# The gate of the first half step on VectorE, and one more chunk in the seven-product form

## The chip, the cores and the metric

One core of one Trainium2 chip. The metric is the device time of one execution in microseconds (us); lower is better. Engines: TensorE (PE, its weight loads PEld), VectorE (DVE), ScalarE (ACT), GpSimd (POOL), SyncE (SP), which issues most transfers.

## The reference

A two-layer backbone over 512 latent tokens and 256 context tokens of width 1024. Each layer is a half SwiGLU step, a token mixer (neighbourhood attention in the first layer, windowed attention in the second) and another half step. Every sub-layer is modulated by vectors made from a conditioning vector, and closed by a layer norm:

```
m_lat = split(silu(c) @ w_mod[i] + b_mod[i], 9)        # context tokens: the same with c_ctx
y = swiglu(h * (1 + scale) + shift, w_in, w_out)       # (silu(a) * v) @ w_out, width 2816
h = layer_norm(ALPHA * h + 0.5 * gate * y)
```

There are four half steps, called 0a, 0b, 1a and 1b. The shift, scale and gate of 0a are the first three of the nine modulation vectors of layer 0 (rows 0 to 7, 8 to 15 and 16 to 23 in blocks of 128 outputs).

## The kernel before

Activations are kept transposed: 8 tiles `z` of 128 features by 768 tokens (512 latent, 256 context). Products are made in three passes, with each operand split into a high and a low part (`mm3`, L152): high by high, low by high, high by low. A weight quarter of 128x512 is loaded raw (`raw_quarter`, L92; five raw buffers), copied to the high part by ScalarE and subtracted to the low part by GpSimd (`split_w`, L100). High and low parts live in a ring of eight quarters each, two units of four.

**A half step** (`ffn`, L457) has 11 chunks of two units of 128 inner features. A plain chunk makes, for each unit f and each group of tokens (512 and 256), `pa` and `pv` (`av`, L465), multiplies `silu(pa)` by `pv` on VectorE, splits the result, and multiplies by the third unit, `down` (L489): 8 output tiles `pd` per group, each added into `z` with the gate as a factor by VectorE (`accumulate`, L452). So the gate must be there before the first addition. The down products of chunk 0 rotate over three banks, two of tag s and the one of tag t.

A chunk in the **seven-product form** (`seven`, L590) makes `pa` and `pv` of both halves of the tokens from seven products instead of eight, as in Strassen's scheme in Winograd's variant. It needs sums of the activations, made once (`sums`, L528, and `fourth`, L549; on VectorE, GpSimd and ScalarE), and sums of the weight quarters for every unit (`quarters`, L566: four additions and seven splits, nearly all on GpSimd). Its down weights are split another way (`adding=True`): ScalarE writes the high part and the negated one, and a transfer on GpSimd's queue adds the weights to it. Before the sums overwrite them, halves of the activations are saved to memory (`save`, L522) and later restored.

`s0` (L638) is the first chunk in that form: 3 in 0a, where the first products were opened already while the inputs came in, and 2 in the others. Chunk `s0 - 1` holds the sums. Chunks 9 and 10 are plain again.

**The modulation vectors** come in two ways. Those of shift and scale of 0a, and its gate, are made on TensorE (`gemv`, L164): weights as the moving operand against a 32-column conditioning operand, evicted and transposed by eight small products with `sel`. For the gate `late_gate` (L1237), called at the start of `ffn` as `mid()`, does two of these with 8 transfers each (`gemv_bg`, L185). All others are **row products on VectorE** (`gemv_dve`, L195): a tile of 128 outputs by 512 inputs is loaded, multiplied by the conditioning row, which lies in a PSUM bank (o for the latent stream, t for the context stream; copied there with Silu by ScalarE, L225), and summed in the same instruction (L208). A block of 128 outputs takes two halves and two streams, four products. They are a background list `bg`; `tick()` (L237) advances it by `pace[0]` steps at fixed places in the chunks. `weight` (L639) says how much each chunk is to take; chunk s0 - 1 takes none. In 0a the list has blocks 24 to 71 of layer 0: 192 products. Outside phase T their rows use the six buffers t2, as the gate's pieces do; in phase T two buffers and `zspare`.

**Order.** The program text gives an order of priority; a planner then simulates the engines and writes each engine's queue, so that an instruction ready early is moved ahead of later ones. Engines take their queues strictly in order. `behind` (L322) adds an order without a wait. `bias_tables` (L822), called at the end of chunk 1 of 0a, builds the attention bias in memory with 8 + 16 transfers of small pieces on SP's queue.

Of the kernel before, what the change touches and what calls it, by code (L numbers as in the profile page):

```python
# [38 lines left out]
def hybrid_kernel(ctx: ExitStack, tc: tile.TileContext, h0, cc, crow, wmod, wmodt, bmod, lnp, wst,  # L39
                  rpbp, nmask, sinks, ropec, rmat, ident, wmask, out):  # L40
    nc = tc.nc
# [8 lines left out]
    def bank(tag, nm):  # L50
        return pp.tile([P, 512], F32, tag=tag, name=nm, bufs=banks[tag])

    def t2(nm, tag="t2"):
        return tp.tile([P, 512], F32, tag=tag, name=nm, bufs={"t2": 6, "ln": 2, "sl": 2}[tag])
# [109 lines left out]
    def gemv(layer, ch, pieces, tag):  # L164

        nm = f"{layer}_{ch}"
        ps = bank(tag, f"gm{nm}")
        kt = 0
        for t in pieces:
            for j in range(t.shape[1]):  # L170
                q = kt % 4
                nc.tensor.matmul(ps[32 * q:32 * q + 32, :], c_sb[:, kt, :], t[:, j, :], start=kt < 4, stop=kt >= 4,
                                 tile_position=(0, 32 * q))
                kt += 1
        ev = t2(f"gev{nm}")
        nc.scalar.copy(ev[:], ps[:])
        pt = bank(tag, f"gt{nm}")
        for j in range(4):
            nc.tensor.matmul(pt[:, 2 * j:2 * j + 2], ev[:, j * P:(j + 1) * P], sel[:], start=True, stop=True)
        for a in range(2):  # L180
            t = ch * 2 + 8 * a if ch < 4 else ch * 4 + 2 * a
            nc.vector.tensor_tensor(out=mod[layer][:, t:t + 2, :], in0=pt[:, 4 * a:4 * a + 4].rearrange("p (t s) -> p t s", s=2),
                                    in1=bmod_sb[:, layer, t:t + 2, None].broadcast_to([P, 2, 2]), op=ALU.add)

    def gemv_bg(layer, ch):  # L185
        pieces = []
        for q in range(8):
            t = t2(f"wm{layer}_{ch}_{q}").rearrange("p (a b) -> p a b", a=1)
            nc.sync.dma_start(t[:], wmod[ch, q // 4, :, q % 4:q % 4 + 1, :])
            pieces.append(t)  # L190
        gemv(layer, ch, pieces, "o")

    bg, last, last_exp, wtq = [], [None], [None], [0]

    def gemv_dve(layer, *ranges):  # L195


        def products(t, half, cb, out):
            wtq[0] += 1
            nm = f"wt{layer}_{t}_{half}"  # L200
            if phase_of[0] != "T":
                w = t2(nm)
            else:
                w = zspare if wtq[0] % 3 == 0 else ph["T"].tile([P, 512], F32, tag="wt", name=nm, bufs=2)
            nc.sync.dma_start(w[:], wmodt[layer, t, half])
            for st in sorted(out):
                junk = t2(f"jk{layer}_{t}_{half}_{st}", "ln")
                x = nc.vector.tensor_tensor_reduce(out=junk[:], in0=w[:], in1=cb[st], scale=1.0, scalar=0.0,  # L208
                                                   op0=ALU.mult, op1=ALU.add, accum_out=out[st])
                behind(x, last[0])  # L210
                yield

        def steps():
            cb, now = {}, None
            for i, (t0, t1, streams) in enumerate(ranges):
                acc = tp.tile([P, 48, 2, 2], F32, tag="gacc", name=f"ga{layer}_{t0}", bufs=1)[:, 0:t1 - t0]
                for half in ((0, 1), (1, 0))[i % 2]:
                    if half != now:
                        now, cb = half, {}
                        for st in streams:  # L220
                            nm = f"cb{layer}_{t0}_{half}_{st}"
                            t = t2(nm, "ln")
                            nc.sync.dma_start(t[:], crow[st, half:half + 1, :].broadcast_to([P, 512]))
                            cb[st] = bank("ot"[st], nm)[:]
                            behind(nc.scalar.activation(cb[st], t[:], AF.Silu), last_exp[0])  # L225
                    for t in range(t0, t1):
                        yield from products(t, half, cb, {st: acc[:, t - t0, half, st:st + 1] for st in streams})
                n = len(streams)
                nc.vector.tensor_tensor(out=acc[:, :, 0, 0:n], in0=acc[:, :, 0, 0:n], in1=acc[:, :, 1, 0:n], op=ALU.add)
                nc.vector.tensor_tensor(out=mod[layer][:, t0:t1, 0:n], in0=acc[:, :, 0, 0:n],  # L230
                                        in1=bmod_sb[:, layer, t0:t1, None].broadcast_to([P, t1 - t0, n]), op=ALU.add)

        bg.append((sum(2 * len(st) * (t1 - t0) for t0, t1, st in ranges), steps()))

    pace = [0.0, 0.0]

    def tick():  # L237

        pace[1] += pace[0]
        while bg and pace[1] >= 1:  # L240
            pace[1] -= 1
            if next(bg[0][1], "end") == "end":
                bg.pop(0)
# [25 lines left out]
    def gate(layer, m, w):  # L269
        gt = cp.tile([P, DT, 2], F32, name=f"gt{layer}_{m}")  # L270
        nc.vector.tensor_scalar(out=gt[:], in0=mvec(layer, m), scalar1=w, scalar2=None, op0=ALU.mult)
        return gt
# [49 lines left out]
    def behind(x, y):  # L322

        if y is not None and x.ins.engine == y.ins.engine:
            tc.add_manual_dep(x.ins, y.ins.name, mybir.DependencyInfo(
                mybir.DependencyClass.NoSync, mybir.DependencyReason.DATA), reason="order")
# [130 lines left out]
    def ffn(nm, groups, gt, mid, post, units=(), opened={}, head=None, apart=None):  # L457
# [177 lines left out]
            mid()  # L635
        gts.append(gt())
        late_downs, js = [], []
        s0 = 3 if opened else 2  # L638
        weight = [0] + [1.0] * (s0 - 2) + [0] + [1.0] * (NCH - 2 - s0) + [1.2] * (s0 - 1)  # L639
        each = sum(n + 1 for n, _ in bg) / (sum(weight) - 0.1)  # L640
        for ci in list(range(NCH)) + [("r", NCH - 2)]:
# [57 lines left out]
            a, b = groups  # L699
# [116 lines left out]
    def constants():  # L816
        for t, src in ((lnp_sb, lnp), (nmask_sb, nmask), (rm_sb, rmat)):
            behind(nc.sync.dma_start(t[:], src[:]), loaded[0])
        nc.sync.dma_start(nsink[:], sinks[:].broadcast_to([P, NH]))
        nc.vector.tensor_scalar(out=nsink[:], in0=nsink[:], scalar1=-1.0, scalar2=None, op0=ALU.mult)  # L820
# [318 lines left out]
    first, opened = [], []  # L1139
# [14 lines left out]
    with tc.tile_pool(name="pre", bufs=1) as fp:  # L1154
        open_av()
        for q in range(4):
            pieces = []
            for i in range(2):
                t = fp.tile([P, 4, 512], F32, tag="wm", name=f"wm0_{q}_{i}", bufs=7)
# [75 lines left out]
            write(norm)  # L1235

    def late_gate():  # L1237
        for ch in (4, 5):
            gemv_bg(0, ch)
        constants()  # L1240

    def whole(x, head):

        return lambda gi: [f() for f in (x[:5] if gi == 0 else head)]
# [4 lines left out]
    l3 = [ln("l3", i, g, 1, 0, 1, 3, "o", True) for i, g in enumerate(g2)]  # L1249
    l4 = [ln("l4", i, g, 1, 1, 1, 6, ("mm", "o")[i]) for i, g in enumerate(g1)]  # L1250

    gemv_dve(0, (24, 40, (0, 1)), (40, 72, (0, 1)))
    ffn("0a", g2, lambda: gate(0, 2, 0.5), late_gate, whole(l0[0], l0[1][:1]), first,
        {(f, g): ps for f in range(2) for g, ps in zip(g2, opened[f])})
    plan(pq0_0_0=l0[1][1:2], pk0_1_0=l0[1][2:3], vn0_1=l0[1][3:5] + l0[0][5:] + l0[1][5:])
# [3 lines left out]
    gemv_dve(1, (0, 24, (0, 1)))  # L1259
    plan(pv0b_0_0_0=l1[1][1:2], pv0b_0_1_0=l1[2][2:3], pd0b_0_0_4=l1[2][3:], pd0b_0_0_7=l1[1][2:3], pa0b_0_0_512=l1[1][3:])  # L1260
    ffn("0b", g2, lambda: gate(0, 8, 0.5), None, whole(l2[0], l2[1][:1]), head=[g3[0], g3[2], g3[1]], apart=True)
    gemv_dve(1, (24, 40, (0, 1)), (40, 72, (0,)))
    plan(pa1a_0_0_0=l2[0][5:], pa1a_0_1_0=l2[1][1:2], pd1a_0_0_1=l2[1][2:3], pd1a_0_0_4=l2[1][3:])
    ffn("1a", g2, lambda: gate(1, 2, 0.5), None, whole(l3[0], l3[1][:1]), apart=True)
    plan(vw_3=l3[1][1:2], wk1=l3[1][2:3], wq0_0=l3[1][3:5] + l3[0][5:] + l3[1][5:])
    plan(wo6_3=l4[0][:1], wo7_2=l4[0][1:2], pow3_1_256_2=l4[0][2:3], pow3_1_256_6=l4[0][3:5], pow3_1_256_7=l4[1][:1])
# [129 lines left out]
```

## Time and profile before

| what | value |
|---|---|
| time, three runs | 2860.63 us median (2854.68 to 2862.81) |
| profiled execution | 2868.23 us, span 2866.4 us |
| busy: PE, DVE, POOL, ACT | 95%, 63%, 58%, 42% |
| mean granted TensorE clock | 0.972 |
| bytes moved | 322.42 MB, mean 112 GB/s |

A row of the timeline gives start and length in us, engine, line, operation, output <- inputs, sizes, count, and in brackets how long the engine was idle before it and what ended that. A row of the windows gives a stretch of the span, its length, the busy time of PE, PEld, DVE, ACT and POOL (with counts), the granted clock, the share of the transfer engines, and GB/s.

### The profile page before, as it was taken

Reading aid. Unit: us, or ns where it says so; the run is one execution under the profiler, and the core shown is the slowest. Engines: PE = TensorE matmul, PEld = TensorE weight load, DVE = VectorE, ACT = ScalarE, POOL = GpSimd, SP = SyncE. Lnnn points to the kernel's source line nnn. Section 1 sums busy time; section 2 is a strip of 40 time slices with the busy share of each in tenths; the row PEclk is TensorE's granted clock in tenths of the full one; section 3 lists DMA queues with packets and bytes.
Section 4 is the critical chain, followed back from the end, with each engine's and each line's share of the span. In section 5 each row is a group of like instructions: output and inputs, shape, how many; then the busy total and the mean of one; then the engine's idle time right before and its main releaser. Section 6 shows DMA issues by size and latency. Waiting matters only on the chain.

```text
span 2866.4 us, 48106 instructions
## 1 busy us (share of the span) xinstructions
PE 2728.1 (95%) x17122; PEld 2447.8 (85%) x17122; DVE 1805.4 (63%) x4124; ACT 1213.4 (42%) x2497; POOL 1658.0 (58%) x1488
## 2 busy tenths in 40 slices
PE   8999999999999989999999999999998998899997
PEld 5789899888888878999998899998886776888997
DVE  3286777585545676766654776666566667687744
ACT  4223333256454444434333534343246555444443
POOL 4357575375434455876744677765466444577763
PEclk9999999999999989999999999999999999899998
DMA  8525557432212212345462326466522111235562
GB/s 300 141 87 158 133 144 208 134 103 82 60 49 62 58 56 86 97 121 140 119 167 83 96 83 166 134 183 180 174 81 62 31 31 45 59 89 129 123 181 65
DMA packets 286016, 322.42 MB, mean 112 GB/s; under 512 B 28497, under 2 KB 174033, under 8 KB 284753
## 3 DMA queue, kind: packets, MB, share of 16 engines
q1 hardware_dynamic: 269936, 290.89, 34.2%
q0 software_dynamic: 15552, 28.32, 5.9%
q8 instruction: 135, 2.21, 0.3%
q14 instruction: 105, 0.85, 0.1%
q10 hardware_dynamic: 288, 0.14, 0.0%
HBM read 311.41 MB, written 12.25 MB: 113 GB/s over the span
## 4 chain that ended last, share of the span: by engine, by line
PE 52%; DVE 6%; DMA 2%; issue 2%; ACT 1%; POOL 1%; SPq 0%; DVEq 0%; POOLq 0%; ACTq 0%
PE pd1a L153 2%; PE pd0b L153 2%; PE pd1a L154 2%; PE pd0b L154 2%; PE pd0b L155 2%; PE pd1a L155 2%; PE wo L800 1%; PE pd1b L153 1%; PE pd1b L154 1%; PE pd1b L155 1%; DMA wr<-in_wst_dram 1%; PE tpw L791 1%; PE pa1a L153 1%; PE pa1a L154 1%; PE pv1a L153 1%
## 5 line engine op out<-in xcount | busy, mean ns | idle before, releaser
L104 POOL TENSOR_TENSOR wl<-wr,wh 128x512 fp32r<-128x512 f32 x308 | 404.0, 1328 | 298.4 <-ACT wh L102 238.4
L104 POOL TENSOR_TENSOR wl_s<-S,wh_s 128x512 fp32r<-128x512 f32 x202 | 268.4, 1366 | 60.5 <-ACT wh_s L102 59.7
L102 ACT CAST wh<-wr 128x512 fp32r<-128x512 f32 x308 | 186.7, 619 | 215.1 <-DMA wr<-in_wst_dram 62.2
L102 ACT CAST wh_s<-S 128x512 fp32r<-128x512 f32 x216 | 130.9, 620 | 322.4 <-POOL S L574 84.1
L208 DVE CUSTOM_DVE_ANT_0 jk<-wt,cb 128x512 f32<-128x512 f32 x303 | 200.4, 680 | 61.4 <-DMA wt<-in_wmodt_dram 52.1
L574 POOL TENSOR_TENSOR S<-wr,wr 128x512 f32<-128x512 f32 x108 | 146.9, 1360 | 148.6 <-DMA wr<-in_wst_dram 130.1
L104 POOL TENSOR_TENSOR wl_a<-wr,wh_a 128x512 fp32r<-128x512 f32 x120 | 159.1, 1376 | 24.9 <-ACT wh_a L102 24.5
L102 ACT CAST wh_a<-wr 128x512 fp32r<-128x512 f32 x162 | 100.4, 621 | 125.9 <-PE pd1b L154 18.3
L453 DVE SCALAR_TENSOR_TENSOR z<-pd0b,gt,z 128x256 f32<-128x256 f32 (+1 forms) x176 | 103.4, 602 | 62.2 <-PE pd0b L155 62.0
L453 DVE SCALAR_TENSOR_TENSOR z<-pd1a,gt,z 128x512 f32<-128x512 f32 (+1 forms) x168 | 99.8, 619 | 44.5 <-PE pd1a L155 43.3
L807 POOL TENSOR_SCALAR p<-p,l 128x512 f32<-128x512 f32 x64 | 44.6, 698 | 128.9 <-DVE l L906 120.5
L453 DVE SCALAR_TENSOR_TENSOR z<-pd0a,gt,z 128x512 f32<-128x512 f32 (+1 forms) x168 | 98.7, 618 | 29.5 <-PE pd0a L155 28.9
L319 POOL TENSOR_SCALAR z<-z,ag_None,ab_None 128x256 f32<-128x256 f32 (+1 forms) x78 | 63.5, 819 | 53.4 <-DVE uh L305 42.8
L208 DVE CUSTOM_DVE_ANT_0 jk<-zspare,cb 128x512 f32<-128x512 f32 x113 | 75.8, 679 | 15.6 <-DMA zspare<-in_wmodt_dram 15.6
L807 POOL TENSOR_SCALAR pw<-pw,l 128x512 f32<-128x512 f32 (+1 forms) x64 | 41.2, 645 | 74.4 <-DVE l L1097 33.0
L574 POOL TENSOR_TENSOR S<-S,wr 128x512 f32<-128x512 f32 x54 | 77.1, 1427 | 3.2 <-DVE x1b L557 0.7
L574 POOL TENSOR_TENSOR S<-wr,S 128x512 f32<-128x512 f32 x54 | 76.8, 1422 | 2.9
L905 ACT ACTIVATE p<-s,m 128x512 f32<-128x512 f32 x64 | 44.0, 688 | 77.3 <-DVE m L903 72.3
L453 DVE SCALAR_TENSOR_TENSOR z<-pd1b,gt,z 128x512 f32<-128x512 f32 (+1 forms) x98 | 56.8, 609 | 14.8 <-PE pd1b L155 12.3
L306 DVE TENSOR_TENSOR ul<-ufl,uh 128x256 fp32r<-128x256 f32 (+1 forms) x88 | 63.0, 722 | 2.3 <-ACT ufl L301 1.7
L301 ACT ACTIVATE ufl<-z,bi_None,sc_None 128x256 f32<-128x256 f32 (+1 forms) x86 | 54.7, 654 | 22.2 <-DVE z L438 21.9
L153 PE MATMUL pd0a<-gh0a,wh 128*128 128x512 f32 (+1 forms) x144 | 50.6, 365 | 8.3 <-DVE z L453 8.3
(1463 smaller groups left out, 10687.0 us busy)
## 6 DMA issues: line engine op xcount, KB each, us to landing
wr<-in_wst_dram SPq DMA_DIRECT2D x524, 256.0 KB
wt<-in_wmodt_dram SPq DMA_DIRECT2D x175, 256.0 KB
zspare<-in_wmodt_dram SPq DMA_DIRECT2D x65, 256.0 KB
wr_0b<-in_wst_dram SPq DMA_DIRECT2D x42, 256.0 KB
wr_1b<-in_wst_dram SPq DMA_DIRECT2D x42, 256.0 KB
wr_2b<-in_wst_dram SPq DMA_DIRECT2D x42, 256.0 KB
wr_3b<-in_wst_dram SPq DMA_DIRECT2D x42, 256.0 KB
wm<-in_wmod_dram SPq DMA_DIRECT2D x8, 1024.0 KB
```

The source lines that it names most:

```text
L102: nc.scalar.copy(hi[:], src[:])
L104: eng.tensor_tensor(out=lo[:], in0=src[:], in1=hi[:].bitcast(F32), op=ALU.subtract)
L153: nc.tensor.matmul(ps, a[0], b[0], start=first, stop=False)
L154: nc.tensor.matmul(ps, a[0], b[1], start=False, stop=False)
L155: last_pe[0] = nc.tensor.matmul(ps, a[1], b[0], start=False, stop=last)
L208: x = nc.vector.tensor_tensor_reduce(out=junk[:], in0=w[:], in1=cb[st], scale=1.0, scalar=0.0, op0=ALU.mult, op1=ALU.add, accum_out=out[st])
L301: nc.scalar.activation(uf[:, :n], zs, AF.Identity, scale=s1, bias=s2)
L306: return hi, nc.vector.tensor_tensor(out=lo, in0=uv, in1=uo.bitcast(F32), op=ALU.subtract)
L319: nc.gpsimd.tensor_scalar(out=zs, in0=zs, scalar1=prm[2][:, d:d + 1], scalar2=prm[3][:, d:d + 1], op0=ALU.mult, op1=ALU.add)
L453: last[0] = nc.vector.scalar_tensor_tensor(out=zt(d, c0, c1), in0=pd, scalar=gt[:, d, st:st + 1], in1=zt(d, c0, c1), op0=ALU.mult, op1=ALU ...
L574: nc.gpsimd.tensor_tensor(out=t[:], in0=a[:], in1=b[:], op=o)
L807: nc.gpsimd.tensor_scalar(out=p, in0=p, scalar1=r, scalar2=0.0, op0=ALU.mult, op1=ALU.add)
```

## The change

Two things change. The gate of 0a is made by `gemv_dve` (blocks 16 to 23, both streams: 32 products), all of it stepped at once in `late_gate`, and `gemv_bg` goes; the background list for blocks 24 to 71 is set up after it, still ahead of chunk 0. And `s0` is 2 in 0a too: chunk 2 takes the seven-product form, chunk 1 holds the sums and takes no background steps, and only chunk 9 instead of 9 and 10 takes them at the end.

```
-    def gemv_bg(layer, ch):
-        pieces = []
-        for q in range(8):
-            t = t2(f"wm{layer}_{ch}_{q}").rearrange("p (a b) -> p a b", a=1)
-            nc.sync.dma_start(t[:], wmod[ch, q // 4, :, q % 4:q % 4 + 1, :])
-            pieces.append(t)
-        gemv(layer, ch, pieces, "o")
...
-        s0 = 3 if opened else 2
+        s0 = 2
...
     def late_gate():
-        for ch in (4, 5):
-            gemv_bg(0, ch)
+        gemv_dve(0, (16, 24, (0, 1)))
+        pace[0] = 1
+        while bg:
+            tick()
         constants()
+        gemv_dve(0, (24, 40, (0, 1)), (40, 72, (0, 1)))
...
-    gemv_dve(0, (24, 40, (0, 1)), (40, 72, (0, 1)))
     ffn("0a", g2, lambda: gate(0, 2, 0.5), late_gate, whole(l0[0], l0[1][:1]), first,
```

## Rows read from the trace of the kernel before

**Rows 1.** The page, busy time of each engine over the whole span.

```profile
PE 2728.1 (95%) x17122; PEld 2447.8 (85%) x17122; DVE 1805.4 (63%) x4124; ACT 1213.4 (42%) x2497; POOL 1658.0 (58%) x1488
```

**Rows 2.** Windows: chunk 2 of 0a, plain, and a seven-product chunk (period).

```profile
161.90:212.10 50.20, 50.20 (x291) 44.28 (x290) 39.55 (x64) 15.90 (x32) 29.64 (x24) 1.00 0.20 61
...
332.90:378.80 45.90, 45.90 (x266) 43.92 (x265) 32.99 (x81) 17.55 (x32) 30.71 (x26) 1.00 0.56 148
```

**Rows 3.** Windows (PE, PEld, clock, DMA) for lines L172 and L179 alone.

```profile
63.00:106.00 43.00, 12.36 (x32) 1.77 (x32) 1.00 0.37 105
...
63.00:106.00 43.00, 1.90 (x16) 2.02 (x16) 1.00 0.37 105
```

**Rows 4.** Timeline of TensorE, around a gate pair and at the first down product.

```profile
63.61 1.05 PE L172 MATMUL gm<-wm,c_sb 128*32 128x512 f32 x2
64.59 0.38 PE L154 MATMUL pa0a<-ul,wh 128*128 128x256 f32 x1
...
74.70 0.39 PE L153 MATMUL pd0a<-gh0a,wh 128*128 128x512 f32 x1
```

**Rows 5.** Timelines of VectorE and SP, and windows, around the wait in chunk 1.

```profile
140.13 0.69 DVE L208 CUSTOM_DVE_ANT_0 jk<-wt,cb 128x512 f32<-128x512 f32 x1 [9.65 <-DMA wt<-in_wmodt_dram]
...
116.46 12.21 SPq L826 DMA_DIRECT2D yd<-xd  x14
129.53 0.87 SPq L205 DMA_DIRECT2D wt<-in_wmodt_dram  x1
...
135.00:142.00 7.00, 0.17 (x2) 0.11 (x1) 1.70 (x5) 0.00 (x0) 0.00 (x0) 0.66 0.89 286
142.00:150.00 8.00, 7.50 (x17) 5.44 (x18) 6.44 (x18) 2.13 (x4) 3.77 (x3) 0.50 0.82 259
```

**Rows 6.** Timelines of VectorE and SP: products back to back, change of half.

```profile
126.58 0.68 DVE L208 CUSTOM_DVE_ANT_0 jk<-wt,cb 128x512 f32<-128x512 f32 x1
127.19 0.08 DVE L208 DVE_READ_ACCUMULATOR2_ANT ga<- 128x1 f32 x1
...
233.32 0.42 SPq L223 DMA_DIRECT2D cb<-in_crow_dram  x1
...
240.40 0.69 DVE L208 CUSTOM_DVE_ANT_0 jk<-wt,cb 128x512 f32<-128x512 f32 x1 [1.90 <-ACT cb L225]
```

**Rows 7.** Timeline of VectorE when the gate is there, and the window before.

```profile
105.61 0.24 DVE L271 TENSOR_SCALAR gt<-mod 128x16 f32<-128x16 f32 x1
...
78.84:105.70 26.86, 26.86 (x142) 18.77 (x141) 2.79 (x9) 5.58 (x11) 8.32 (x8) 1.00 0.31 93
```

**Rows 8.** GpSimd: the page's group of a split, and an accumulate transfer's issue.

```profile
L104 POOL TENSOR_TENSOR wl_s<-S,wh_s 128x512 fp32r<-128x512 f32 x202 | 268.4, 1366 | 60.5 <-ACT wh_s L102 59.7
...
305.19 0.87 POOL L107 DMA_DIRECT2D wl_3b<-in_wst_dram  x1
```

**Rows 9.** Timelines and windows: the waits in chunks 3 and 4.

```profile
259.82 0.69 DVE L208 CUSTOM_DVE_ANT_0 jk<-zspare,cb 128x512 f32<-128x512 f32 x1 [4.34 <-DMA zspare<-in_wmodt_dram]
...
318.82 0.79 PE L153 MATMUL pd0a<-gh0a,wh_2b 128*128 128x512 f32 x1 [6.89 <-DVE gl0a L603]
...
306.48 8.37 DVE L260 TENSOR_TENSOR bi_None<-sc_None,lnp_sb 128x16 f32<-128x16 f32 x1
...
306.20:312.00 5.80, 5.72 (x26) 4.38 (x24) 5.80 (x2) 1.67 (x3) 5.80 (x5) 1.00 0.45 94
...
226.70:332.90 106.20, 95.68 (x529) 89.51 (x529) 77.98 (x173) 36.49 (x68) 67.72 (x57) 0.95 0.51 142
```

**Rows 10.** Windows: the turn to the seven-product form in 0b.

```profile
1150.00:1170.00 20.00, 18.84 (x109) 16.16 (x108) 19.76 (x34) 5.99 (x14) 10.26 (x9) 1.00 0.00 1
```

**Rows 11.** Groups of VectorE between 162 and 212 us: two kinds of sums.

```profile
L518 DVE TENSOR_TENSOR x0a<-x0a,ul 128x384 f32<-128x384 f32 x12 | 6.7, 560 | 0.2
L559 DVE TENSOR_TENSOR ul<-x0a,uh 128x384 fp32r<-128x384 f32 x4 | 4.4, 1119 | 0.0
```

**Rows 12.** Timeline of TensorE: the longest wait of the second mixer.

```profile
2435.59 0.58 PE L153 MATMUL pow<-woh,wh 128*128 128x256 f32 x1 [8.44 <-ACT pw L1084]
```

## The prediction, made before the changed kernel was run

> **What bounds the kernel now.** I read the page first: TensorE is busy 95% of the span and no other engine passes 63% [rows 1]. So an instruction taken off TensorE's queue is worth its own time, and one put on another engine costs only where TensorE comes to wait for it. Next I read the windows of the first half step, stage by stage. A plain chunk lasts 50.20 us and a chunk in the seven-product form 45.90 us, TensorE busy throughout in both [rows 2]. Then I looked for what else stands in that stage. There are three things: the gate's own matmuls, which lie among the others [rows 3]; one long wait at chunk 1's down product [rows 5]; and shorter waits in chunks 3 and 4, where VectorE waited for rows of the modulation weights or for its turn [rows 9].
>
> **Part 1, the gate leaves TensorE.** Removed are 32 gate matmuls and 16 small transposing ones: 12.36 + 1.90 us of TensorE time between 63 and 106 us [rows 3]. They displace other work: a pair begins at 63.61, lasts 1.05, and the next product follows at 64.59 [rows 4]. So all 14.3 us count: **-14.3**. The 16 weight transfers of 256 KB on SP's queue are replaced by 16 of the same size, plus four short-issue loads of the conditioning row; the transfer engines were 37% busy there [rows 3], so I cost the bytes at nothing. ScalarE loses two copies and gains four Silu passes of the same width, also nothing. What is added is VectorE's: 8 row groups x 2 halves x 2 streams = 32 products. Product and accumulator read repeat every 0.61 us [rows 6], so 19.5 us. VectorE worked only 2.79 of the 26.86 us before the gate now arrives [rows 7], so this lies in idle time.
>
> When is the new gate ready? The first gate piece of the old form was multiplied at 63.61 [rows 4]; the new rows go through the same buffers. From there 16 products are 9.8 us, a change of half costs about 7 us (conditioning row asked for at 233.32, second stream's first product at 240.40 [rows 6]), 16 more are 9.8, and the sums about 1: **91 us** (an estimate from these rows), where it is 105.61 now [rows 7]. Until then TensorE can run chunk 1's first products, as it does now up to about 105; without the 14.3 us of gate work it reaches that point at 91. Cover and gate meet, and I take 0 for this wait. If the cover is gone, the price is rival A.
>
> **Part 2, chunk 2 in the seven-product form.** TensorE: 50.20 - 45.90 [rows 2], **-4.3**. VectorE does 22 short operations on the products instead of 8. GpSimd goes from 12 operations to 22 of 1.366 us, plus four accumulate transfers issued in 0.87 us each [rows 8], some 17 us more. ScalarE makes 22 instead of 12 casts or copies of weights. SP's queue carries 12 loads either way, and GpSimd's queue gains the four. In the steady seven-product chunk, which holds all of this, it is hidden: GpSimd is busy 30.71, VectorE 32.99 and ScalarE 17.55 of 45.90 [rows 2]. The background products, 193 steps with their closing one, now start in chunk 2 and end in chunk 9: 23.8 per chunk instead of 20.75, 1.9 us more on VectorE, hidden likewise. Chunk 10's down product returns to three banks; its six matmuls of a group of 512 take longer than one accumulation, nothing.
>
> **Part 3, the wait at chunk 1.** VectorE stood 9.65 us for a row of weights, from 130.5, because the row was asked for at 129.53, behind 14 issues of the bias tables [rows 5]. TensorE then idled 6.8 of the 7 us from 135, and ran at a granted clock of 0.50 (1.2 instead of 2.4 GHz) from 142 to 150, 7.50 us of work worth half [rows 5]. That is 6.8 + 0.5 + 3.8 = 11.1 us. Chunk 1 now has no background products (its weight is zero), so this wait has nothing left to hang on: **-11.1**; the bounds are -11.1 and 0, if another wait takes its place.
>
> What is late next? Chunk 1 takes over the sums, the save of the latent halves and the fourth sum, and chunk 2's weights are asked for while the bias tables are still moving. Both sides have a row. The second half step has the same order (two plain chunks, then seven): TensorE loses 1.16 us there, with VectorE at 19.76 of 20 [rows 10], but without bias tables. The other end is 40 us, rival B. I take **+1.2** for the order and **+4.3** for one late transfer like that of 259.82 [rows 9], the commonest size of such a wait in this stage. The waits of chunks 3 and 4 (6.89 us and shorter [rows 9]) I leave. From 226.70 to 332.90 two chunks' work takes 106.2 us [rows 9], which is 91.8 at the rate of rows 2, so 14.4 us are lost; more steps per chunk argue for more, a later start for fewer.
>
> **Sum.** -14.3 - 4.3 - 11.1 + 1.2 + 4.3 = **-24.2**. The profiled execution took 2868.2 us around a span of 2866.4, 7.6 above the median; it would become 2844.0. Against the median of 2860.6 the forecast is **2836.4**.
>
> **One rule weighed.** Among the sums, those that read two tiles of SBUF last longer than those with one operand in PSUM while GpSimd works: 1.119 us in the group that suffers most, against 0.560 [rows 11], a mean loss of 0.56. A tiny one of 16 columns took 8.37 us, GpSimd being busy 5.80 of 5.80 in its first part [rows 9]. The Trainium skill, page "SBUF — State Buffer", section "Who interferes with whom", says that such a VectorE operation and a GpSimd one that reads SBUF exclude each other, the second waiting until the first has finished. By that rule alone each loss is up to one GpSimd operation; the 8.37 shows several in a row. This makes rival C.
>
> **Rivals.** *A: the order on TensorE is written for an earlier gate.* The order is planned, and the plan had VectorE's rows land too early at 130.5 [rows 5]. If the downs of chunk 0 stand ahead of chunk 1's products, TensorE is done with its own work at 74.7, its first down product now [rows 4], less 6.4 (six gate pieces) and plus 2.8 (what two banks take), so 71 and waits 20 us for 91, plus about 4 at half clock as in rows 5: -24.2 + 24 = 0, **2860**. For: the rows come late in a crowded queue. Against: the present plan fills that time without one wait. Chance 0.15.
>
> *B: slower.* Place: chunk 2's first products. Its eight weight quarters go through five raw buffers while the bias tables move; a row took from 129.53 to 140.13 to arrive [rows 5], so two rounds are 21, and eleven GpSimd operations of 1.36 us are 15 more. TensorE idles 36 us and loses 4 by the clock; the present wait is gone all the same: -29.7 + 40 = +10, **2870.9**. It decides from 38.3 us of new loss on. For: GpSimd's fifteen are as long as TensorE's work on a unit, about a third of the 45.90 of rows 2. Against: the tables also come some 14 us earlier. Chance 0.10.
>
> *C: the sums wait for GpSimd.* Twelve two-tile sums and four of their splits each wait 1.36 us, 21.8 on a VectorE that has no slack at this turn [rows 10]: 2836.4 - 1.2 + 21.8 = **2857** at the full price, 2846 at half. For: the 8.37. Against: even the worst group of rows 11 loses 0.56 a time. Chance 0.10.
>
> *D: little comes of it.* The whole order is planned anew, and later stages have waits up to 8.44 us that hang on a single instruction [rows 12]; two more of that size give **2853**. Chance 0.06.
>
> *E: more.* The waits of chunks 3 and 4 go too: 2836.4 - 14.4 = **2822**. Chance 0.14.
>
> **The numbers.** The forecast keeps 0.45, in a range of its own of 2828 to 2849 (no late transfer and one of the present ones gone, or four late ones). A measurement of this kernel tells about 0.3%, 8.6 us, from no change. Faster than 2852: the forecast, E, half of C, a third of D and a fifth of A, 0.71. Slower than 2869: B, 0.10. The rest, 0.19, within. The range runs from 2818 (E with nothing late at chunk 2) to 2862 (A): B stays outside, and with it what takes more than one of these mechanisms.
>
> **What would show it.** Gate matmuls between 60 and 106 us gone, the first product p0 of the half step 56 instead of 48 per line, VectorE's row products 448. The gate multiplied at 85 to 95 us. No wait over 5 us between 90 and 150, and granted clock 1.00 there. The end of the half step earlier by 24 us, the stages behind it as long as before. The prediction is wrong if TensorE waits at chunk 0's down product for the gate, or at the first p products for weights, or if the half step's gain is not found again at the end.

## The result, and the profile of the changed kernel

| | before | changed |
|---|---|---|
| median of four runs each | 2861.72 us (2854.68 to 2866.77) | 2833.90 us (2828.75 to 2838.70) |
| ratio, 95% interval | 1 | 0.9903 [0.9879, 0.9927] |
| profiled execution, span | 2868.23, 2866.4 us | 2832.82, 2830.4 us |
| mean granted clock | 0.972 | 0.982 |

The change is worth 27.8 us; 24.2 was forecast. Later runs of the same changed kernel gave 2833.04 us, 0.9904 [0.9885, 0.9923], and a second trace, whose longest wait between 90 and 150 us is again 9.49 us. The two profiled executions lie 35.4 us apart, because the one before was 6.5 above its median and this one 1.1 below: 27.8 + 6.5 + 1.1. Lines of the program have moved up by 8 (the gate is L263 now, L271 before).

The page's engine line, against [rows 1]:

```profile
PE 2691.7 (95%) x17050; PEld 2427.2 (86%) x17050; DVE 1825.0 (64%) x4200; ACT 1221.7 (43%) x2511; POOL 1674.0 (59%) x1502
```

TensorE is 36.4 us less busy, which is more than the 18.6 of parts 1 and 2: the mean clock rose too, and work done at half the clock is busy for twice as long.

Timeline of VectorE: the first row product of the gate, the first after the change of half, the gate, and the first of the sums that are made in the two banks s.

```profile
58.63 0.68 DVE L200 CUSTOM_DVE_ANT_0 jk<-wt,cb 128x512 f32<-128x512 f32 x1
...
76.30 0.69 DVE L200 CUSTOM_DVE_ANT_0 jk<-wt,cb 128x512 f32<-128x512 f32 x1 [4.88 <-ACT cb L217]
...
90.94 1.21 DVE L263 TENSOR_SCALAR gt<-mod 128x16 f32<-128x16 f32 x1
...
117.54 0.56 DVE L510 TENSOR_TENSOR x0a<-uh 128x384 f32<-128x384 f32 x1
```

The gate is there at 90.94 instead of 105.61 [rows 7]. Now the timeline of TensorE, at its first down product and at its one long wait of the half step's start:

```profile
65.54 0.40 PE L153 MATMUL pd0a<-gh0a,wh 128*128 128x512 f32 x1
...
141.74 0.79 PE L153 MATMUL pd0a<-gh0a,wh 128*128 128x512 f32 x1 [9.49 <-DVE T0a_3l L536]
```

And the windows (columns as in the section on the profile of before): while the gate is made, the wait, the 10 us behind it, and two seven-product chunks as in the last of [rows 9].

```profile
66.00:90.00 24.00, 24.00 (x135) 20.98 (x134) 18.12 (x56) 6.68 (x13) 12.11 (x12) 1.00 0.55 174
...
132.00:142.00 10.00, 0.51 (x3) 0.27 (x2) 9.81 (x20) 3.86 (x8) 4.98 (x5) 0.66 0.00 0
142.00:152.00 10.00, 9.12 (x43) 7.56 (x44) 5.78 (x8) 4.56 (x8) 9.84 (x9) 0.83 0.24 71
...
208.20:307.20 99.00, 94.51 (x531) 88.35 (x530) 71.06 (x179) 34.77 (x65) 68.75 (x58) 0.98 0.58 150
```

The first shows what part 1 hoped for: VectorE works 18.12 of 24 us and TensorE does not notice. The second and third are the price of the turn to the new form: 9.49 us idle while VectorE works 9.81 of 10, and a granted clock of 0.50 (1.2 GHz) for 10.2 us. Most of that stretch lies in the wait itself, as its own window shows:

```profile
135.10:145.34 10.24, 3.60 (x9) 2.83 (x10) 8.53 (x15) 2.94 (x7) 6.12 (x6) 0.50 0.00 0
```

Only 3.6 us of it are work, which at the full clock would have been half of that. So the clock adds 1.8 us, and the turn costs 11.3. The last window of the four is 7.2 us shorter than the 106.20 before.

The wait in chunk 1 [rows 5] is gone. SyncE's queue and ScalarE's at that place:

```profile
97.14 1.96 SPq L94 DMA_DIRECT2D wr<-in_wst_dram  x2
...
100.32 15.10 SPq L818 DMA_DIRECT2D yd<-xd  x16
```

```profile
112.99 1.39 ACT L102 CAST wh_a<-wr 128x512 fp32r<-128x512 f32 x2
116.67 0.86 ACT L472 CAST gh0a<-pv0a 128x512 fp32r<-128x512 f32 x2 [2.29 <-PE pd0a L154]
```

Two weight loads were asked for ahead of the 16 table transfers, and the casts ahead of `gh0a` on ScalarE's queue found their weights there.

A second piece of the gain lies where the prediction had put nothing: from the end of chunk 8's down product to the first `v` product of the attention. Before, then changed:

```profile
502.00:637.40 135.40, 129.67 (x693) 111.75 (x692) 96.17 (x211) 51.83 (x91) 74.14 (x61) 0.97 0.40 120
```

```profile
481.80:607.20 125.40, 125.04 (x693) 108.88 (x692) 75.01 (x168) 52.49 (x91) 75.79 (x62) 1.00 0.37 108
```

The same 693 rows of TensorE take 10.0 us less. VectorE is 21.2 us less busy, the clock is full and the waits are gone.

### The profile page after: what moved, and what is told of

The parts are those of the page before. It is cut to its first block, busy times and chain, and to the rows that moved or that the text cites. A ratio compares the mean times of both kernels' runs of the same rounds, so it can differ in the third digit from the quotient of the medians.

```text
span 2830.4 us, 48091 instructions
## 1 busy us (share of the span) xinstructions
PE 2691.7 (95%) x17050; PEld 2427.2 (86%) x17050; DVE 1825.0 (64%) x4200; ACT 1221.7 (43%) x2511; POOL 1674.0 (59%) x1502
## 4 chain that ended last, share of the span: by engine, by line
PE 78%; DVE 10%; DMA 5%; issue 3%; ACT 2%; POOL 1%; SPq 0%; DVEq 0%; ACTq 0%; POOLq 0%
DMA wt<-in_wmodt_dram 2%; PE pd0b L153 2%; PE pd0b L154 2%; PE pd0b L155 2%; PE pd1a L153 2%; PE pd1a L154 2%; PE pd1a L155 2%; PE pd0a L153 1%; PE wo L792 1%; PE pd0a L154 1%; PE pd0a L155 1%; PE o L792 1%; PE pd1b L153 1%; DVE jk L200 1%; PE pd1b L154 1%
## 5 line engine op out<-in xcount | busy, mean ns | idle before, releaser
L104 POOL TENSOR_TENSOR wl<-wr,wh 128x512 fp32r<-128x512 f32 x296 | 389.8, 1332 | 255.2 <-ACT wh L102 219.1
L104 POOL TENSOR_TENSOR wl_s<-S,wh_s 128x512 fp32r<-128x512 f32 x210 | 277.7, 1359 | 45.7 <-ACT wh_s L102 34.1
L102 ACT CAST wh<-wr 128x512 fp32r<-128x512 f32 x296 | 179.6, 621 | 194.2 <-DMA wr<-in_wst_dram 53.7
L200 DVE CUSTOM_DVE_ANT_0 jk<-wt,cb 128x512 f32<-128x512 f32 x325 | 214.4, 681 | 36.6 <-DMA wt<-in_wmodt_dram 31.7
L104 POOL TENSOR_TENSOR wl_a<-wr,wh_a 128x512 fp32r<-128x512 f32 x126 | 166.9, 1371 | 18.3 <-ACT wh_a L102 18.1
L200 DVE CUSTOM_DVE_ANT_0 jk<-zspare,cb 128x512 f32<-128x512 f32 x123 | 83.0, 681 | 42.4 <-DMA zspare<-in_wmodt_dram 31.4
L153 PE MATMUL vn<-wh,uh 128*128 128x256 f32 x192 | 54.8, 285 | 0.0
(1463 smaller groups left out, 10632.3 us busy)
```

The costliest lines, as they stand in the source:

```text
L102: nc.scalar.copy(hi[:], src[:])
L104: eng.tensor_tensor(out=lo[:], in0=src[:], in1=hi[:].bitcast(F32), op=ALU.subtract)
L153: nc.tensor.matmul(ps, a[0], b[0], start=first, stop=False)
```

## The experiments

Each kernel was run in five rounds beside the kernel before on the same chip; the ratios are to that one, whose median was 2857.86 to 2861.68 us. A gain in us that is worked out from a ratio is 2860 times its distance from 1; differences to the changed kernel are of medians, against its 2833.04.

**The gate alone.** The changed kernel, with the old start of the new form:

```
-        s0 = 2
+        s0 = 3 if opened else 2
```

> The gate by row products, chunk 2 plain as before (s0 = 3). Theory (the gain is a sum: 14.3 us of gate work off TensorE, 4.3 by the form of chunk 2, 11.1 because chunk 1 takes no background rows): only the first term, -14 us against the kernel before, and TensorE still waits in chunk 1, 5 us or more, with VectorE standing for a row of weights. No wait for the gate. Rival (the gate's matmuls lay in time that TensorE had to spare): 0 to -3 us.

Measured: 2843.74 us, 0.9951 [0.9939, 0.9964], which is 14.0 us (10.3 to 17.4). The gate is worth what its matmuls took. The wait in chunk 1 stayed. Timelines of SyncE, ScalarE and TensorE in this kernel:

```profile
100.02 1.92 SPq L94 DMA_DIRECT2D wr<-in_wst_dram  x2
103.34 15.31 SPq L818 DMA_DIRECT2D yd<-xd  x16
...
129.62 0.62 ACT L102 CAST wh<-wr 128x512 fp32r<-128x512 f32 x1 [12.66 <-DMA wr<-in_wst_dram]
...
130.78 1.65 PE L153 MATMUL pd0a<-gh0a,wh 128*128 128x512 f32 x3 [10.89 <-ACT gh0a L472]
```

TensorE waited for `gh0a`, which stood on ScalarE's queue behind the cast of a weight that came 12.66 us late. So it isn't only VectorE's background row that comes late there.

**The chunk alone.** The kernel before, the gate on TensorE as it was:

```
-        s0 = 3 if opened else 2
+        s0 = 2
```

> The gate on TensorE as before, chunk 2 in the seven-product form (s0 = 2). Theory: -4.3 by the form, -11.1 for the wait that goes, about +14 for the wait at the turn (9.5 idle and the clock), and about -10 because no background rows are left for chunk 10: -11 us. Rival (the whole gain comes from where the background rows lie): -25 us or more. Rival (the wait at the turn eats all): 0.

Measured: 2863.05 us, 1.0018 [1.0005, 1.0032], which is 5.1 us slower (1.4 to 9.2) where 11 faster was expected. Chunk 1 took no background rows, and it waited all the same. Timelines of SyncE, ScalarE and TensorE in this kernel:

```profile
115.76 15.16 SPq L826 DMA_DIRECT2D yd<-xd  x16
131.55 7.47 SPq L94 DMA_DIRECT2D wr<-in_wst_dram  x4
...
142.13 0.62 ACT L102 CAST wh_a<-wr 128x512 fp32r<-128x512 f32 x1 [10.40 <-DMA wr<-in_wst_dram]
...
143.53 0.80 PE L153 MATMUL pd0a<-gh0a,wh 128*128 128x512 f32 x1 [6.53 <-DVE gl0a L481]
...
164.90 0.80 PE L153 MATMUL pd0a<-gh0a,wh 128*128 128x512 f32 x1 [9.07 <-DVE T0a_3l L544]
```

This refutes my reason for the -11.1: without rows of the modulation weights, a weight quarter behind the tables takes their place. The wait at the turn (164.90) belongs to the new form too, not to the gate. And the change is more than the sum of its halves: alone they are worth 14.0 and -5.1 us, together 27.8. Each half alone still waits behind the tables (10.89 and 6.53 us), and both together don't; how much of the difference that is, the runs don't split.

**The tables out of the way, in the kernel before.** Instead of 16 transfers in a row at the end of chunk 1, two after each unit of the chunks in the new form:

```
-        for h in range(NH):
-            nc.sync.dma_start(yd[h], ...)
+        def one(h):
+            behind(nc.sync.dma_start(yd[h], ...), loaded[0])
+        later.extend(lambda h=h: one(h) for h in range(NH))
...
                     seven(f"{nm}_{ci}_{i}", wpos[0] + i, *gs[i])
+                    for _ in range(min(2, len(later))):
+                        later.pop(0)()
```

> The kernel before, with the 16 transfers that build the attention bias spread over chunks 3 to 7, two after each unit, instead of all at the end of chunk 1. Theory now (the wait in chunk 1 belongs to whatever is asked for behind these transfers: a background row or a weight quarter): the wait of 6.8 us goes, with its half-speed stretch, 11 us faster than the kernel before, about 2849; the 135 us from the last down of chunk 8 to the attention's v products stay. Rival (the prediction's: it is the background rows of chunk 1): those are all there, so a wait of 5 us or more stays, 2857 to 2862.

Measured: 2846.07 us, 0.9945 [0.9925, 0.9964], so 15.7 us (10.3 to 21.5). Windows over chunk 1's down products, in the kernel before and in this one:

```profile
133.40:162.10 28.70, 21.37 (x100) 17.50 (x99) 19.23 (x48) 4.36 (x9) 7.15 (x6) 0.76 0.65 205
```

```profile
134.20:153.00 18.80, 17.96 (x100) 14.79 (x99) 16.98 (x44) 3.91 (x8) 6.99 (x6) 1.00 0.60 193
```

The same 100 rows of TensorE take 18.80 instead of 28.70 us, all background rows in place, the clock full. The cause of the wait in [rows 5] was the block of table transfers. **The same in the changed kernel**, which no longer has that wait:

> The changed kernel with the bias transfers spread in the same way over chunks 2 to 6. Theory (in the changed kernel nothing that chunk 1 needs stands behind them, and the wait of 9.5 us at the turn is VectorE's load): no change, 2834 within 4 us, the wait at the turn 9 to 10 us. Rival (the turn waits for weights that stand behind them): the wait at the turn goes, 2820.

Measured: 2836.75 us, 0.9917 [0.9899, 0.9936], not told apart from the changed kernel. The wait at the turn stays as long, in the timeline of TensorE:

```profile
142.11 0.79 PE L153 MATMUL pd0a<-gh0a,wh 128*128 128x512 f32 x1 [9.49 <-DVE T0a_3l L536]
```

So rival B's mechanism, weights of chunk 2 behind the tables, isn't what costs at the turn.

**Part of the sums on GpSimd.** In the changed kernel's 0a, twelve operations of the sums go from VectorE to GpSimd (the low part of the third sum, and the last addition and the low part of the fourth):

```
-                y = nc.vector.tensor_tensor(out=lo, in0=x, in1=hi.bitcast(F32), op=ALU.subtract)
+                move = bool(opened) and i == 2
+                y = (nc.gpsimd if move else nc.vector).tensor_tensor(out=lo, in0=x, in1=hi.bitcast(F32), op=ALU.subtract)
...
-                nc.vector.tensor_tensor(out=x, in0=x, in1=y, op=ALU.add)
+                eng = nc.gpsimd if opened else nc.vector
+                eng.tensor_tensor(out=x, in0=x, in1=y, op=ALU.add)
...
```

> The changed kernel with 12 of the sums' operations in 0a (the low parts of the third sum and the two additions of the fourth) on GpSimd instead of VectorE. Theory (the wait of 9.5 us at the turn is VectorE's load, 9.81 of 10 us busy there): VectorE has 6.6 us less to do, the wait falls to about 3 us and the half-speed stretch after it with it; 8 us faster than the changed kernel, about 2826. Rival (GpSimd then is late with chunk 2's weights): the wait moves to the first products, 2834 or more.

Measured: 2845.56 us, 0.9956 [0.9940, 0.9971], 12.5 us slower than the changed kernel. A miss, but a telling one. Timelines of SyncE, ScalarE and TensorE:

```profile
100.07 0.64 SPq L94 DMA_DIRECT2D wr<-in_wst_dram  x1
...
129.75 0.62 ACT L102 CAST wh_a<-wr 128x512 fp32r<-128x512 f32 x1 [13.12 <-DMA wr<-in_wst_dram]
...
130.90 1.65 PE L153 MATMUL pd0a<-gh0a,wh 128*128 128x512 f32 x3 [10.60 <-ACT gh0a L472]
```

With other costs the planner wrote other queues: one weight load ahead of the tables (which follow at 103.34, for 15.07 us) instead of two, and the wait in chunk 1 was back. In the changed kernel its absence is a matter of the order that came out.

**The sums freed from the banks.** In the changed kernel's 0a, the first two sums go to SBUF instead of the two PSUM banks s, and are not held to the written order of VectorE:

```
-            x1, x2 = [bank("s", ...)[:, 0:n2] if paced else t2(...)[:, 0:n2] for i in range(2)]
+            x1, x2 = [bank("s", ...)[:, 0:n2] if paced and not opened else t2(...)[:, 0:n2] for i in range(2)]
...
-            if paced:
+            if paced and not opened:
                 behind(x, last[0])
```

> The changed kernel, with the sums of 0a free to run before chunk 0's last additions: their first two tiles in SBUF instead of the PSUM banks of tag s, and no order behind the last addition. Theory (the turn waits because 22 us of sums on VectorE start only at 117.5, and hold both banks s until they end): VectorE does them in its idle time from 80 to 117, the wait of 9.5 us and the half-speed stretch after it go, 12 to 14 us faster than the changed kernel, about 2821. Rival (the rule on two SBUF operands: 20 more of these operations wait for GpSimd): they lengthen by half a microsecond or more each, a wait of 5 us or more stays, 2830.

Measured: 2837.02 us, 0.9912 [0.9890, 0.9934]: no gain, as the rival said, though not with one long wait. The wait at the turn is gone, but others have come, the longest of 4.69 us at 121.50. TensorE's waits between 90 and 150 us add up to 11.7 us, in the changed kernel to 11.5. The window from 90 to 120 us in this kernel:

```profile
90.00:120.00 30.00, 23.11 (x115) 19.06 (x113) 30.00 (x41) 8.19 (x17) 20.83 (x17) 0.94 0.61 165
```

Its timeline of TensorE:

```profile
121.50 0.58 PE L153 MATMUL pd0a<-gh0a,wh 128*128 128x256 f32 x1 [4.69 <-DVE z L445]
```

Its groups of VectorE from 90 to 152 us (busy us and mean ns behind the bar):

```profile
L551 DVE TENSOR_TENSOR ul<-x0a,uh 128x384 fp32r<-128x384 f32 x4 | 4.6, 1146 | 0.0
L549 DVE TENSOR_TENSOR x0a<-x0a,x0a 128x384 f32<-128x384 f32 x4 | 4.5, 1131 | 0.0
L510 DVE TENSOR_TENSOR x0a<-uh 128x384 f32<-128x384 f32 x3 | 4.4, 1463 | 0.0
```

The same groups in the changed kernel:

```profile
L549 DVE TENSOR_TENSOR x0a<-x0a,x0a 128x384 f32<-128x384 f32 x4 | 3.3, 818 | 1.3 <-POOL x0a L548 1.3
...
L551 DVE TENSOR_TENSOR ul<-x0a,uh 128x384 fp32r<-128x384 f32 x4 | 2.6, 660 | 0.6 <-ACT uh L550 0.6
L510 DVE TENSOR_TENSOR x0a<-uh 128x384 f32<-128x384 f32 x4 | 2.5, 614 | 0.0
```

VectorE is busy 30.00 of 30 us from 90 to 120. The operations of L551 and L549, which are the same in both kernels, take 1.7 and 1.4 times as long; the first sum (L510) takes 2.4 times as long, but it now also writes SBUF instead of PSUM. GpSimd works 20.83 of these 30 us, and only 7.64 of the 24.5 us from 117.50 on, where the changed kernel makes most of its sums.

**The gate's products twice.** In the changed kernel every row product of the gate is made a second time into a scratch tile, 32 more of about 0.6 us:

```
+                if layer == 0 and 16 <= t < 24:
+                    junk = t2(f"jk2{layer}_{t}_{half}_{st}", "ln")
+                    nc.vector.tensor_tensor_reduce(out=junk[:], in0=w[:], in1=cb[st], ..., accum_out=out[st])
```

> The changed kernel with each of the 32 gate products made twice (same result, 19.5 us more on VectorE). Theory (the gate at 91 just meets the end of what TensorE can do without it): the gate comes at about 110, TensorE has some 8 us more of chunk 1's second unit to do and then waits 10 us, losing 4 to 5 more by the clock; 15 us slower than the changed kernel, about 2849. Rival (the planner finds cover for that too): 3 us or less.

Measured: 2861.95 us, 1.0012 [0.9998, 1.0025], 29 us slower than the changed kernel and nearly twice the 15 expected. Timelines of VectorE, TensorE, SyncE and ScalarE:

```profile
113.79 0.93 DVE L267 TENSOR_SCALAR gt<-mod 128x16 f32<-128x16 f32 x1
...
112.66 0.76 PE L153 MATMUL pd0a<-gh0a,wh 128*128 128x512 f32 x1 [5.67 <-DVE ga L205]
...
131.00 0.80 PE L153 MATMUL pd0a<-gh0a,wh 128*128 128x512 f32 x1 [12.28 <-DVE z L449]
...
99.47 15.27 SPq L822 DMA_DIRECT2D yd<-xd  x16
...
122.37 2.97 SPq L219 DMA_DIRECT2D cb<-in_crow_dram  x2
...
128.66 0.60 ACT L221 ACTIVATE cb<-cb 128x512 f32<-128x512 f32 x1 [14.38 <-DMA cb<-in_crow_dram]
```

The gate comes 22.85 us later, and two waits follow. In the first, TensorE stood 5.67 us for the last of the gate's products. The second and longer one, 12.28 us to 131.00, isn't the gate's: VectorE, with the additions behind, stood 13.09 us for a cast of ScalarE, and ScalarE stood 14.38 us for a conditioning row of the background list, which was asked for at 122.37 behind the 16 table transfers. The granted clock was 0.50 from 109.0 to 115.8 and from 122.7 to 136.3, with 3.2 and 5.3 us of work in these stretches. So in this run, where the gate comes 23 us later, nothing is left of the change's gain, which is the size of rival A; but a good part of that loss is the table block again, and how much reserve the cover has for the gate alone this run doesn't show.

**Where the background rows end.** In the changed kernel they are spread over chunks 9 and 10, as before the change:

```
-        weight = [0] + [1.0] * (s0 - 2) + [0] + [1.0] * (NCH - 2 - s0) + [1.2] * (s0 - 1)
+        t0 = 3 if opened else 2
+        weight = [0] + [1.0] * (s0 - 2) + [0] + [1.0] * (NCH - 2 - s0) + [1.2] * (t0 - 1)
```

with `t0` for `s0` also where chunk 10 decides whether it takes rows and gives its down product all banks.

> The changed kernel with the background rows spread over chunks 9 and 10 again, at 20.75 a chunk instead of 23.8. Theory (the 10 us gained after chunk 8 come from the rows that no longer stand among chunk 10 and the layer norm): 7 to 10 us slower than the changed kernel, about 2843, the stages from chunk 9 to the attention's first product that much longer. Rival (those 10 us are scatter between executions): 2834, within 3 us of the changed kernel.

Measured: 2841.91 us, 0.9955 [0.9938, 0.9972], 8 to 9 us slower than the changed kernel by medians, 15 by the ratios, whose intervals don't overlap. Window of the same stretch as above:

```profile
481.80:616.80 135.00, 129.96 (x694) 112.72 (x693) 94.12 (x212) 52.70 (x93) 74.42 (x61) 0.96 0.40 118
```

It begins at the same 481.80 us and takes 135.00, as in the kernel before. **The reverse, in the kernel before:** the rows end in chunk 9 (`t0 = 2`, with `s0` as it was).

> The kernel before with its background rows ended in chunk 9 instead of chunk 10 (22.5 a chunk instead of 20.75); nothing else is changed. Theory (the last part of the step is 10 us shorter when no background row stands among chunk 10 and the layer norm): 125 instead of 135 us from the last down of chunk 8 to the attention's v products, 8 to 10 us faster than the kernel before, about 2851. Rival (only the seven-product form of chunk 2 brings it): 135 us, no change.

Measured: 2850.69 us, 0.9968 [0.9956, 0.9980], 9.2 us (5.7 to 12.6) faster, and the stretch is 125.40 long:

```profile
501.10:626.50 125.40, 125.04 (x692) 108.84 (x692) 74.92 (x168) 52.28 (x91) 75.71 (x62) 1.00 0.34 108
```

(The pace of this kernel is 23.8 steps a chunk, not 22.5: 193 steps over weights of 8.1.) Two edits, one each way, give and take the 10 us. Which half does it, the rows in chunk 10 or its down product over all banks, wasn't tried.

The same pair of kernels shows what the pace of the rows does earlier. Windows over chunks 5 to 8 of the changed kernel (23.8 steps a chunk; its chunks 3 and 4 took 99.00), then over chunks 3 and 4 and chunks 5 to 8 with the rows spread (20.75). Each stretch ends with the down product of its last chunk:

```profile
307.20:481.80 174.60, 170.46 (x973) 160.19 (x972) 125.78 (x307) 65.08 (x119) 103.54 (x87) 1.00 0.64 174
```

```profile
207.90:312.20 104.30, 94.40 (x530) 88.82 (x530) 74.36 (x164) 35.43 (x67) 69.50 (x59) 0.95 0.52 142
312.20:481.80 169.60, 169.05 (x973) 160.74 (x973) 120.05 (x287) 65.13 (x119) 101.56 (x86) 1.00 0.63 171
```

The faster pace wins 5.3 us in chunks 3 and 4 and loses 5.0 in chunks 5 to 8. In the kernel before, chunks 5 to 8 took 168.90, and 174.90 with its rows ended early. What is won hangs on one operation, that of 16 columns and 8.37 us in [rows 9]. Timelines of VectorE, changed kernel and rows spread:

```profile
272.25 0.23 DVE L252 TENSOR_TENSOR bi_None<-sc_None,lnp_sb 128x16 f32<-128x16 f32 x1
```

```profile
286.54 8.43 DVE L252 TENSOR_TENSOR bi_None<-sc_None,lnp_sb 128x16 f32<-128x16 f32 x1
```

It takes 0.22 or 0.23 us in all nine traces of kernels with 23.8 steps a chunk, and 7.67 to 8.54 us in the four with 20.75, where TensorE then waits 5.43 to 7.92 us. GpSimd was busy 8.33 of the 8.37 us in the kernel before.

**The sums in other banks.** In the changed kernel's 0a, the first two sums take banks o and t, and chunk 0's down product the banks s alone, with the freer order:

```
-            x1, x2 = [bank("s", ...)[:, 0:n2] if paced else ...
+            x1, x2 = [bank("ot"[i] if opened else "s", ...)[:, 0:n2] if paced else ...
...
-            if paced:
+            if paced and not opened:
...
-... "sss" if ci == 0 and apart else "sst")
+... "sss" if ci == 0 and (apart or opened) else "sst")
```

> The changed kernel with the sums of 0a free to run from the gate on, but with their first two tiles in the PSUM banks o and t (free between the two uses by the row products), and chunk 0's down on the two banks s alone. Theory (the turn waits because the sums start late; moving them early in SBUF was eaten by their waits for GpSimd, and in PSUM they do not wait): the sums fill VectorE's idle time from 91 to 117 at about 0.56 us each, the waits between 90 and 150 fall below 3 us in all, 10 to 14 us faster than the changed kernel, about 2822. Rival (VectorE's work before the turn is what bounds, wherever its operands lie): 2834, the waits moved to chunk 0's down.

Measured: 2830.08 us, 0.9894 [0.9877, 0.9912], the lowest median of all, but not told apart from the changed kernel's 0.9903 and 0.9904. The long wait at the turn is gone (the longest between 90 and 150 us is 2.29, and all of them add up to 3.0), yet the down product of chunk 8 ends at 481.52 instead of 481.82. The gain went back in chunk 2's down product: 25.4 us of window, where the changed kernel took 17.4. Timeline of VectorE:

```profile
192.65 0.69 DVE L200 CUSTOM_DVE_ANT_0 jk<-wt,cb 128x512 f32<-128x512 f32 x1 [5.01 <-DMA wt<-in_wmodt_dram]
```

Window of that down product:

```profile
186.90:212.30 25.40, 19.46 (x100) 15.59 (x99) 17.48 (x40) 5.52 (x11) 18.30 (x15) 0.93 0.63 176
```

VectorE stood at a background row that hadn't come, with the additions of the down product behind it on its queue. **Fewer rows there:** the last kernel, with half the background steps in chunk 2.

```
+        if opened:
+            weight[s0] = 0.5
```

> The kernel with the sums in banks o and t, whose chunk 2 is given half as many background steps (weight 0.5 instead of 1.0; the other chunks take about 7% more each). Theory: with the turn free, what chunk 2's down product lost (25.3 us instead of 17.4, behind a row that VectorE awaited for 5.01 us) hung on the number of rows asked for there: the down of chunk 2 back at 17 to 18 us, the long wait at the turn still gone, time 2830 - 7 = about 2823 us. Rival: rows come late wherever the transfers are at their limit, and chunk 3 or 4 loses what chunk 2 wins: about 2830 us, with a wait of 3 us or more of VectorE for a row in chunk 3 or 4. Slower than 2836 would mean that the higher pace of the later chunks costs more than it brings.

Measured: 2834.08 us, 0.9917 [0.9899, 0.9935]: the rival. Timelines of VectorE and TensorE:

```profile
183.95 0.69 DVE L200 CUSTOM_DVE_ANT_0 jk<-wt,cb 128x512 f32<-128x512 f32 x1 [6.09 <-DMA wt<-in_wmodt_dram]
...
234.73 0.69 DVE L200 CUSTOM_DVE_ANT_0 jk<-wt,cb 128x512 f32<-128x512 f32 x1 [6.56 <-DMA wt<-in_wmodt_dram]
...
281.85 6.49 DVE L252 TENSOR_TENSOR bi_None<-sc_None,lnp_sb 128x16 f32<-128x16 f32 x1
...
295.17 0.77 PE L153 MATMUL pd0a<-gh0a,wh_3b 128*128 128x512 f32 x1 [4.64 <-DVE z L445]
```

Chunk 2's down product shortened to 19.3 us, but VectorE now waits for a row in chunks 2, 3 and 4 (3.82 us in the last, to 280.63), and chunk 4's down product took 26.1 us. Not all of that is late rows: the operation of 16 columns takes 6.49 us here, 0.22 in the kernel with the sums in banks o and t. What would keep the turn's 11.3 us stays open.

## Why the prediction held, step by step

The forecast was 2836.4 us with a range of 2818 to 2862; 2833.9 came. That the sum fits so well is luck in part. The turn cost 5.8 us more than forecast and the faster pace of the rows 5.7, while chunks 3 and 4 gave 7.2 and the end of the half step 10.0; the last three had been put at nothing.

| step | forecast | what the runs showed |
|---|---|---|
| gate's matmuls off TensorE | -14.3 | -14.0 (10.3 to 17.4), gate alone |
| gate ready | 91, wait 0 | 90.94, no wait |
| chunk 2's form | -4.3 | not measured alone |
| wait in chunk 1 | -11.1 | gone; 9.9 between the windows, 15.7 (10.3 to 21.5) by the tables' run |
| turn to the new form | +5.5 | 9.49 idle and 1.8 by the clock: +11.3 |
| waits of chunks 3 and 4 | 0 | 106.20 to 99.00: -7.2 |
| more background steps in chunks 5 to 8 | 0 | 168.90 to 174.60: +5.7 |
| chunk 10 and end of the rows | 0 | 135.40 to 125.40: -10.0 |

With 9.9 for chunk 1 the right column adds up to -28.7 in the traces, -14.3 and -4.3 being taken as forecast; at the attention's first `v` product the two traces stand 637.46 against 607.20, -30.3. This can't be set against the 27.8 between the medians to the last microsecond: from that product on, where the program text is the same, single traces of this case took between 2218 and 2232 us (2229 before, 2223 here).

Of the signs that the prediction named, the gate's time and the counts came (56 products per line, 448 row products). "No wait over 5 us between 90 and 150, and granted clock 1.00 there" did not: the turn's wait is 9.49 us, at 0.50.

**Part 1 held throughout.** The 32 products began earlier than I had put them (58.63, not 63.61) and were not back to back, and the change of half cost 4.88 of idle time; they took 32.3 us to the gate where I had 27.6, and the end was the same. That the planner would move the cover was the right reading: TensorE's first down product came at 65.54, the rest of its work up to 90 us was made without a wait, and rival A did not come.

**Part 3's first step failed in its reason.** "Chunk 1 now has no background products, so this wait has nothing left to hang on" named one customer of a blocked queue for the cause. The chunk alone had none of them and still waited 6.53 us. [Rows 5] held the right reading, in the row of 14 table transfers that took 12.21 us to issue: for what is asked behind them an engine stood 9.65, 10.40, 12.66, 13.12 and 14.38 us in five kernels, be it for a row of either kind or a weight, and each time TensorE came to wait behind it. The wait went because two weight loads were ordered ahead of the tables and ScalarE's casts ahead of `gh0a` needed no later one; with one load ahead, or one cast more, it was there again. The gain in the forecast was had, but by this order. That I kept 0 as its other end was the right caution.

**The turn was mis-sized.** From the half step with the same order [rows 10] I took 1.2, and for the rest a late transfer, 4.3. The loss was 11.3, and no transfer made it: the transfer engines stood at a share of 0.00 from 132 to 142 us. VectorE was the bound, 9.81 of 10. In 0a it starts the first of the sums in the banks s only at 117.54, behind chunk 0's last addition; and the sums hold those banks, which the next down product needs. The run with the sums in banks o and t took this wait away, so its cause is those banks and the written order, together; they weren't tried apart. Why 0a pays so much more than 0b isn't shown. The gate's time alone doesn't set it: with the gate there at 90.94, at 104.84 (the chunk alone) and at 113.79 (the products twice) the wait was 9.49, 9.07 and 9.49. But the order that I called the same is not: 0b takes chunk 0 group by group (`apart=True`), each group's down product behind its own products, where 0a writes all products first.

**"Hidden likewise" was wrong for the rows' pace.** I costed 23.8 steps a chunk instead of 20.75 as 1.9 us more on VectorE and put nothing for TensorE. Chunks 5 to 8 took 5.7 us longer, and with the rows spread again they took 169.60.

**Chunk 10 was costed at nothing.** I looked at its banks, and at the rows' new end only for the steps per chunk, not for what leaves chunk 10. VectorE was busy 96.17 us of that stretch, 75.01 now. TensorE's waits there and the clock of 0.97 could be read in a window of the trace before, but I had read the first half step only up to chunk 4.

**Rivals.** B (weights behind the tables) did not come: spreading the tables changed nothing. C was not the likeliest, but its price is real, where sums read two tiles of SBUF beside GpSimd: 660 to 1146, 818 to 1131 and 614 to 1463 ns. The Trainium skill, page "SBUF — State Buffer", section "Who interferes with whom", says that such a VectorE operation and a GpSimd one that reads SBUF exclude each other; the trace agrees, in a mean loss of 0.3 to 0.85 us. Half of E came, 7.2 of 14.4, and most of it because the operation of 16 columns no longer fell beside a busy GpSimd, which I had not foreseen. D and A did not come. (The parts named for "faster than 2852" add up to 0.69, not 0.71.)

## What to carry to other kernels

When an engine waits for a late transfer, ask what stands ahead of it on the queue, not who asked: taking that customer away puts the next one in its place, and moving the block is what helped here, by 15.7 us. A price read at the same turn elsewhere holds only if the order and the buffers around it are the same: 1.2 us in 0b were 11.3 in 0a. Read a change to the end of its loop, since background work that ends a chunk earlier gave 10 us here where nothing else was changed; and count on a wait removed ahead of in-order queues being handed back at the next late transfer, until a run shows otherwise.

## What the runs showed of the hardware that was not expected

- A wait of TensorE can cost more than its length, and the clock can fall within the wait: in the changed kernel TensorE stopped at 132.2, the granted clock was 0.50 from 135.1 to 145.3 us, and work began again at 141.74, so 3.6 us of it ran at half speed. In the last kernel, at the end of a wait of 4.64 us, it was 0.50 from 294.6 to 298.0.
- Sixteen table transfers in a row take 15.1 to 15.3 us to issue, and a 256 KB load asked for right behind them at 131.55 was first cast at 142.13 us. In the changed kernel two such loads asked for ahead of them were cast without a wait.
- A VectorE operation on 16 columns of two tiles in SBUF took 0.22 or 0.23 us in nine traces and 6.49 to 8.54 in five; in the kernel before it was 8.37, with GpSimd busy 8.33 of them. Operations on 384 columns took 1.4 to 1.7 times as long in the run that put the sums in SBUF, where GpSimd was busier beside them.
